# First-group tiles, input order and buffers in a one-core hybrid encoder layer on Trainium2

## The chip, the cores and the metric

The program runs on one core of one Trainium2 chip. The metric is the device time of one execution in microseconds (us), taken as the median of several runs. A core has the engines TensorE (PE, matrix products; PEld is its weight load), VectorE (DVE), ScalarE (ACT), GpSimd (POOL) and SyncE (SP, which here only issues transfers), and 16 DMA engines that serve all queues.

## The reference

One layer for 256 new positions (prompt) and 32 running ones (sample), 288 columns in all, float32, 2048 model channels:

```python
xn   = rmsnorm(x, norm_mix_pre)
proj = xn @ w_in                     # u 1024 | z 2048 | xBC 2560 | dt 32
pool = trailing means of u over windows 2/4/8/16, minus u, @ w_pool per group of 256, * pool_scale
ssd  = Mamba-2 mixer: conv of width 4 and silu on xBC, chunked scan with dt,
       * silu(z), rmsnorm over each of 2 groups of 1024 channels, * ssd_norm
x    = x + rmsnorm(concat[pool, ssd] @ w_out, norm_mix_post)
x    = x + rmsnorm(ConvFFN(rmsnorm(x, norm_ffn_pre)), norm_ffn_post)
```

The outputs are both x and the new histories and states of the pool, the convolutions and the scan.

## The kernel before

**Products.** Activations are kept as 128-channel tiles of 288 columns. Every float32 product is made of three products in a reduced format: weights and activations are each split into a high and a low part, and high x high, high x low and low x high are summed (`mm3`, L162 to L164). ACT makes the high part of the weights (`whi`, L156), DVE the low part (`wlo`, L157), in pieces of 128x1024. `project` (L167) fetches the weights of some output columns (`fetch_w`, L139, on SP), splits them and multiplies; a projection of 256 columns over 16 input tiles is 96 products and four splits on each of ACT and DVE.

**The first group (L217 to L475).** The input isn't there at first, so the kernel starts differently. The 16 input tiles are taken in ten chunks (`CHUNKS`: four of one tile, six of two). For each chunk `first_load` (L238) fetches 800 columns of `w_in` into a slot `raw` (4 slots), with two transfers (L242: B, C and dt; L243: 256 further columns). `prepare` (L363) splits them on ACT (L374, L375) and DVE (L397 for the first four chunks, L388 for the rest), scales and splits the input tile (L372 or L383 on ACT, L390 on DVE), copies it to `xT` (L395) and issues the load of the chunk four further on. For chunks 0 to 3 the input `x0`, `x0s` (512 channels in token order) is turned by PE (`turn_first`, L351, L355, L356); for the others DVE turns it (L378) from `xt`, loaded at L236 and L260. Squares of the input for its norm are taken on ACT with `junk` as their output (L407, L409). The products (L475) go to seven accumulators `first`: 0 and 1 (xs tiles 0 and 1, in the PSUM pool `aux` of three slots), 2 to 5 (B and C) and 6 (dt). `keep_busy` (L337) issues products on a constant tile, whose result is not used: 10 at the start, 5 ahead of the first chunk. Four times parameters are turned by PE through the one `aux` slot left (`columns`, L320) and copied by ACT (L426, L429, L432).

**The rest of the mixer.** `conv_in` (L500) takes a PSUM tile, scaled by the row norm `rstd`, into one of four buffers `ebuf` (L505, L506); `conv_out` (L510) does the convolution and silu on DVE and ACT (L516 to L524). The order in the program is: B, C and xs tiles 0, 1 from the first group; projections xs1 to xs7 (two tiles each), z0 to z7, then u3, u2, u1, u0. Each xs tile goes through `blocks_out` (L195: a DVE transpose into the single buffer `blocks` and four transfers to DRAM) and is read back by `ssd_quad` (L656), which does the scan for four heads at a time. `gate_in` takes z out of PSUM (L771), `gate_mul` (L779) multiplies it in and adds squares to `gsum` on POOL (L762). `rstd_all` sums `gsum` over channels with PE (L740) and makes the group's norm: rg0 for tiles 0 to 7, placed behind z4; rg1 for tiles 8 to 15, placed behind the first u projection.

**The pool mixer.** `pool_in` (L861) takes a u tile into one of four buffers `ubuf` (L864, L865); these are allocated and cleared (L853) after the mixer's buffers are given up. `pool_tile` (L869) makes the window sums and the difference `du`, `pool_group` (L892) multiplies it by `w_pool`. Then the normed xs tiles are split into `mixs` (L124, L125), which take the slots of the 16 `xn` tiles, and `w_out` follows.

**What sets the order.** Each engine works through its instructions in one order. A builder puts them in that order by priority (program order, unless `high_priority` moves them) and by its own simulation of when inputs are ready, so PE instructions of one step can stand inside another's. `pin` keeps an instruction in program order; the whole first group is pinned. In the built program, transfers from SP and ACT share eight completion counters, taken in turn, so an issue waits for the transfer eight before it.

Of the kernel before, what the change touches and what calls it, by code (L numbers as in the profile page):

```python
# [8 lines left out]
F32 = mybir.dt.float32  # L9
F32R = mybir.dt.float32r  # L10
AF = mybir.ActivationFunctionType
ALU = mybir.AluOpType
# [4 lines left out]
P = 128  # L17
# [3 lines left out]
NS = 32  # L21
# [23 lines left out]
CHUNKS = ((0, 1), (1, 1), (2, 1), (3, 1), (4, 2), (6, 2), (8, 2), (10, 2), (12, 2), (14, 2))  # L45
BUSY = 10


@with_exitstack
def body(  # L50
# [57 lines left out]
    def aux(shape, name):  # L108
        return aux_ps.tile(shape, F32, tag="aux", name=name)
# [97 lines left out]
    ones = const.tile([P, P], F32, name="ones")  # L207
    pool.memset(ones, 1.0)
    start = ExitStack()
    xin = start.enter_context(tc.tile_pool(name="xin", bufs=1))  # L210
# [7 lines left out]

    x0 = xin.tile([P, 2, 4 * P], F32, name="x0")
    x0s = xin.tile([NS, 4 * P], F32, name="x0s")  # L220
    xt = xin.tile([P, 9, 3, P], F32, name="xt")
# [16 lines left out]
    def first_load(kb, n):  # L238

        raw = wpool.tile([P, n, NW], F32, tag="raw", name="raw")  # L240
        src = win0[:, kb : kb + n] if kb < 4 else win[:, kb // 4, kb % 4 : kb % 4 + n]
        pin(sp.dma_start(out=raw[:, :, 2 * P :], in_=src[:, :, O_B : O_B + NW - 2 * P]))  # L242
        pin(sp.dma_start(out=raw[:, :, : 2 * P], in_=src[:, :, O_X : O_X + 2 * P]))  # L243
        raws.append(raw)
# [4 lines left out]
    first_input(sp, 0, 0)  # L249
    first_input(act, 1, 0)  # L250
    pin(act.dma_start(out=x0s, in_=x_sample[0, :, 0 : 4 * P]))
    first_load(*CHUNKS[0])
    first_input(sp, 0, 1)
    first_input(sp, 1, 1)
    first_load(*CHUNKS[1])
    first_load(*CHUNKS[2])
# [29 lines left out]
    for i in range(NE):  # L286
# [6 lines left out]
        in_=norm_mix_pre[0, 4 * P :].rearrange("(c p j) -> p c j", p=P, j=4),  # L293
    )
    pb_in = xin.tile([108, P], F32, name="pb_in")
    pool.dma_start(out=pb_in[0:60, :], in_=rows4(state_ssd_conv))
# [37 lines left out]
    def keep_busy(n):  # L334

        for _ in range(n):
            pin(pe.matmul(first[1], busy[:, 0:P], busy, start=True, stop=True))  # L337

    keep_busy(BUSY)
    p_ = aux([P, 4], "pt")  # L340
    pin(pe.transpose(p_, g_in, ident[:4, :4]))
    pin(dve.tensor_copy(g_mix_pre[:, 0:4], p_))
    ssum = xin.tile([P, 12], F32, name="ssum")
    junk = xin.tile([P, 4 * P], F32, name="junk")
    sel4 = xin.tile([P, NS], F32, name="sel4")
# [6 lines left out]
    def turn_first(t):  # L352
        p_ = aux([P, NT], "pt")
        for b in range(2):
            pin(pe.transpose(p_[:, b * P : (b + 1) * P], x0[:, b, t * P : (t + 1) * P], ident))  # L355
        pin(pe.transpose(p_[:, NP_:], x0s[:, t * P : (t + 1) * P], ident[:NS, :NS]))  # L356
        return p_

    def prepare(i, p_=None):
# [6 lines left out]
        tiles = range(kb, kb + n)  # L366
        pieces = (slice(2 * P, NW), slice(0, 2 * P)) if i == 0 else (slice(0, NW),)
        for t in tiles:
# [7 lines left out]
        for t in tiles:  # L376
# [5 lines left out]
            if i:  # L382
                pin(act.activation(  # L383
                    xn[t][:, 0, :], xT[t] if p_ is None else p_, AF.Copy, scale=g_mix_pre[:, t : t + 1]
                ))
        if p_ is None:
            for c in pieces:
                pin(dve.tensor_tensor(lo[:, :, c], raw[:, :, c], hi[:, :, c].bitcast(F32), op=ALU.subtract))  # L388
        for t in tiles:
# [3 lines left out]
            ))  # L393
        if p_ is not None:
            pin(dve.tensor_copy(xT[kb], p_))  # L395
            for c in pieces:
                pin(dve.tensor_tensor(lo[:, :, c], raw[:, :, c], hi[:, :, c].bitcast(F32), op=ALU.subtract))  # L397
        if i + 4 < len(CHUNKS):
# [18 lines left out]
    p_ = turn_first(0)  # L417
    keep_busy(5)
    ahead_w = [prepare(0, p_)]
    for i, (kb, n) in enumerate(CHUNKS):  # L420
# [40 lines left out]
        for q, (r, m, k, x) in enumerate(products):  # L461
            if q == 10 and i < 3:
                ahead_w.append(prepare(i + 1, turn_first(i + 1)))
            if i == 8 and q in (0, 24):
                p_ = aux([P, 3, NF * 2], "ptf")
                for j in range(3):
                    pin(pe.transpose(p_[:, j, :], pf_in[:, q // 8 + j, :], ident[: NF * 2, : NF * 2]))
                pin(act.activation(pf[:, q // 8 : q // 8 + 3, :], p_, AF.Copy))
            if r is None:
                out, c, r = first[6][: 2 * HEADS, :], w[:, k, NW + NB :], 0  # L470
                stop = x == 1
            else:
                out, c = first[m], w[:, k, r * NW + m * P :][:, :P]
                stop = r == 1
            pin(pe.matmul(out, c, xn[kb + k][:, x, :], start=kb + k + r + x == 0, stop=kb + k == KD - 1 and stop))  # L475
# [34 lines left out]
    def conv_out(i, e, out):  # L510
# [13 lines left out]
        dve.scalar_tensor_tensor(out[:, NP_:], th[:, 259:], 1.0, c[:, 259:], op0=ALU.add, op1=ALU.mult)  # L524


    v = mp.tile([HEADS, NT], F32, tag="z", bufs=4, name="v")
# [6 lines left out]

    xs_ps = [first[:2], project(win, [(O_X + 256, 256)], xn, K16, wait=last_split)]
    xT_f = xT_d.rearrange("c p j n -> (c p j) n")
# [274 lines left out]
    for i in range(1, NX // 2):  # L811
        xs_evac(i, xs_ps[i] if i == 1 else project(win, [(O_X + 256 * i, 256)], xn, K16))
        xs_conv(i - 1)
        run_quads(XS_RATE[i])
# [29 lines left out]

    ups = [project(win, [(768, 256)], xn, K16)]
    rg.append(rstd_all(gsum[1], 0.25 / 1024, "rg1"))
    mixer.close()
    outp = ExitStack()
    op_ = outp.enter_context(tc.tile_pool(name="outp", bufs=1))
    ubuf = []  # L850
    for i in range(4):
        e = op_.tile([P, 350], F32, name=f"ubuf{i}")
        pool.memset(e, 0.0)  # L853
        ubuf.append(e)
    uin = {}
    mix = [None] * (NU + NX)
    n_u = [0]
    u_of = {}

    def pool_in(i, p_):  # L860
        u = u_of[i] = ubuf[n_u[0] % 4]  # L861
        n_u[0] += 1
        with tc.high_priority(offset=EVAC):
            dve.tensor_tensor(u[:, 15:271], p_[:, :NP_], rstd[:, :NP_], op=ALU.mult)  # L864
            dve.tensor_tensor(u[:, 286:318], p_[:, NP_:], rstd[:, NP_:], op=ALU.mult)  # L865
        pool.tensor_copy(u[:, 271:286], hist_u[:, :, i])

    def pool_tile(i):
# [185 lines left out]
    x1d = dram.tile([NT, D_MODEL], F32, name="x1d")  # L1054
    outp.close()


# [291 lines left out]
```

## Time and profile before

| what | value |
|---|---|
| median of 3 runs | 1354.79 us (1353.28 to 1355.25) |
| profiled execution | 1361.21 us |
| its span, first to last instruction | 1359.3 us |
| mean granted TensorE clock | 0.997 |
| PE busy in 0 to 66 us | 61.1 us |
| end of the first group's products | 59.4 us |
| DVE busy in 59 to 236 us | 159.7 of 177 us |
| DMA mean rate over the span | 185 GB/s |

Times in the profile count from the first instruction of the profiled execution. A row of the timeline gives start, duration, engine, line, operation, output and inputs, and in brackets how long the engine sat idle before it and what released it. PE's products overlap: the spacing of their starts says how fast PE runs, not their duration. A matmul that is shown with 0.29 us starts 0.131 us after the one before.

### The profile page before, as it was taken

The numbers are of one execution on the slowest core, as the hardware profiler recorded it, in microseconds if no ns is written. First come the engines' busy times: TensorE is split into PE (matmuls) and PEld (weight loads), VectorE is DVE, ScalarE is ACT, GpSimd is POOL, SyncE is SP. The second block draws the span as 40 slices with busy tenths as digits, with TensorE's granted clock in tenths as the row PEclk, the third lists the DMA queues.
The fourth block names the chain that finished last, engine by engine and source line by source line (L and its number), as shares of the span: only waits on it lengthen the run. The fifth ranks groups of instructions, "written<-read, shape, count | busy, mean of one in ns | idle before, by whom it ended". The sixth has DMA issues, their size and how long they took to land.

```text
span 1359.3 us, 25801 instructions
## 1 busy us (share of the span) xinstructions
PE 1342.0 (99%) x10180; PEld 1328.6 (98%) x10180; DVE 889.6 (65%) x1509; ACT 672.6 (49%) x1028; POOL 235.4 (17%) x395
## 2 busy tenths in 40 slices
PE   8999998999999999999999999999999999999997
PEld 7999998999999999999999999999999999999997
DVE  5798889769634469977676653335666666664454
ACT  5755957445544356644544433334444444454443
POOL 3132112111223230211221100000211211101110
PEclk9999999999999999999999999999999999999999
DMA  9878885556755645867555455555455455576763
GB/s 255 259 202 246 267 233 162 170 185 191 222 182 183 191 142 151 250 187 207 160 171 170 150 168 171 164 167 174 157 171 170 158 175 165 159 235 181 196 172 102
DMA packets 302944, 252.13 MB, mean 185 GB/s; under 512 B 74708, under 2 KB 295410, under 8 KB 302822
## 3 DMA queue, kind: packets, MB, share of 16 engines
q1 hardware_dynamic: 300270, 245.63, 59.9%
q0 software_dynamic: 2352, 4.66, 1.2%
q8 instruction: 79, 1.29, 0.4%
q14 instruction: 43, 0.35, 0.1%
q10 hardware_dynamic: 200, 0.20, 0.0%
HBM read 236.13 MB, written 14.31 MB: 184 GB/s over the span
## 4 chain that ended last, share of the span: by engine, by line
PE 91%; DMA 4%; DVE 2%; SPq 1%; issue 1%; ACT 1%; POOL 0%; DVEq 0%; ACTq 0%; POOLq 0%
PE acc L162 29%; PE acc L164 29%; PE acc L163 28%; DMA xs_d<-blocks 2%; DMA raw<-in_w_in 1%; PE acc L475 1%; PE pst L980 1%; SPq L202 1%; PE acc L1255 1%; DVE wlo L157 1%; PE acc_x L475 0%; DMA xt<-in_x_prompt 0%; DMA xk<-xs_d 0%; DVE m L679 0%; PE py L691 0%
## 5 line engine op out<-in xcount | busy, mean ns | idle before, releaser
L157 DVE TENSOR_TENSOR wlo<-raw,whi 128x1024 fp32r<-128x1024 f32 (+1 forms) x402 | 479.8, 1195 | 342.1 <-ACT whi L156 341.0
L156 ACT ACTIVATE whi<-raw 128x1024 fp32r<-128x1024 f32 (+1 forms) x402 | 413.5, 1031 | 481.6 <-PE acc L163 401.6
L162 PE MATMUL acc<-hn,whi 128*128 128x288 f32 x1376 | 404.1, 295 | 0.0
L163 PE MATMUL acc<-hn,whi 128*128 128x288 f32 x1376 | 403.6, 294 | 0.3 <-DVE hn L1039 0.3
L164 PE MATMUL acc<-hn,wlo 128*128 128x288 f32 x1376 | 403.1, 294 | 0.0
L163 PEld LDWEIGHTS acc<-hn,whi 128*128 128x128 f32 x1376 | 259.7, 189 | 0.7 <-DVE hn L1039 0.7
L164 PEld LDWEIGHTS acc<-hn,wlo 128*128 128x128 f32 x1376 | 259.6, 189 | 0.0
L162 PEld LDWEIGHTS acc<-hn,whi 128*128 128x128 f32 x1376 | 257.2, 187 | 0.1
L162 PE MATMUL acc<-fa,whi 128*128 128x288 f32 x682 | 201.9, 296 | 0.0
L163 PE MATMUL acc<-fa,whi 128*128 128x288 f32 x682 | 201.9, 296 | 0.0
L164 PE MATMUL acc<-fa,wlo 128*128 128x288 f32 x682 | 201.5, 295 | 0.0
L164 PE MATMUL acc<-xn,wlo 128*128 128x288 f32 x608 | 179.7, 296 | 1.6 <-DVE wlo L157 1.6
L162 PE MATMUL acc<-xn,whi 128*128 128x288 f32 x608 | 181.1, 298 | 0.2 <-DVE ebuf L506 0.2
L163 PE MATMUL acc<-xn,whi 128*128 128x288 f32 x608 | 180.6, 297 | 0.0
L163 PEld LDWEIGHTS acc<-fa,whi 128*128 128x128 f32 x682 | 128.6, 188 | 0.0
L162 PEld LDWEIGHTS acc<-fa,whi 128*128 128x128 f32 x682 | 128.1, 188 | 0.0
L164 PEld LDWEIGHTS acc<-fa,wlo 128*128 128x128 f32 x682 | 127.9, 188 | 0.0
L164 PEld LDWEIGHTS acc<-xn,wlo 128*128 128x128 f32 x608 | 115.5, 190 | 2.6 <-DVE wlo L157 2.3
L163 PEld LDWEIGHTS acc<-xn,whi 128*128 128x128 f32 x608 | 115.7, 190 | 0.3
L162 PEld LDWEIGHTS acc<-xn,whi 128*128 128x128 f32 x608 | 114.7, 189 | 0.8 <-issue 0.4
L1073 POOL COPY fc_stage<-ebuf 128x4 f32<-128x4 f32 x88 | 27.3, 310 | 496.9 <-DVE ebuf L1072 453.5
L1068 POOL COPY ebuf<-pf 128x2 f32<-128x2 f32 x88 | 72.0, 818 | 129.6 <-DVE fc L1079 58.9
(355 smaller groups left out, 1790.6 us busy)
## 6 DMA issues: line engine op xcount, KB each, us to landing
raw<-in_w_up SPq DMA_DIRECT2D x80, 1024.0 KB, 5.2
raw<-in_w_in SPq DMA_DIRECT2D x76, 512.0 KB, 5.0
raw<-in_w_down SPq DMA_DIRECT2D x32, 1024.0 KB, 5.3
raw<-in_w_out SPq DMA_DIRECT2D x24, 1024.0 KB, 5.5
raw<-in_w_down SPq DMA_DIRECT2D x16, 768.0 KB, 4.8
raw<-in_w_up SPq DMA_DIRECT2D x14, 512.0 KB, 4.4
gb<-g_d SPq DMA_DIRECT2D x8, 832.0 KB, 7.5
raw<-in_w_in SPq DMA_DIRECT2D x6, 544.0 KB, 6.6
```

Source lines behind the costliest of these rows:

```text
L156: act.activation(hi, raw[:, k : k + n, :], AF.Copy)
L157: dve.tensor_tensor(lo, raw[:, k : k + n, :], hi.bitcast(F32), op=ALU.subtract)
L162: then(pe.matmul(out, wh, a[:, 0, :], start=start, stop=False))
L163: then(pe.matmul(out, wh, a[:, 1, :], start=False, stop=False))
L164: then(pe.matmul(out, wl, a[:, 0, :], start=False, stop=stop))
L202: sp.dma_start(out=dv[i], in_=s[32 * i : 32 * (i + 1), :].rearrange("r (j f) -> r j f", f=32))
L475: pin(pe.matmul(out, c, xn[kb + k][:, x, :], start=kb + k + r + x == 0, stop=kb + k == KD - 1 and stop))
L980: ins = pe.matmul(st[:, o, :], x_, btok[:, gi, b, :], start=b != 1, stop=b != 0)
L1068: pool.tensor_copy(e[:, 258:260], pf[:, 4:6, i])
L1073: pool.tensor_copy(fc_stage[:, :, :, i], e[:, 256:324].rearrange("p (s c) -> p s c", c=34)[:, :, 0:2])
L1255: pin(pe.matmul(o, hi, f2[k][:, :, c], start=k == 0, stop=end, skip_group_check=True))
```

## The change

It does these things:

- The 256 further columns that the first group makes are now u tiles 6 and 7 (the pool mixer's last two) and no longer xs tiles 0 and 1. They are taken out of PSUM right behind B and C by `pool_in`, into `ubuf`, which now is allocated and cleared at the start, in a pool of its own that stays open through the mixer. xs0 becomes an ordinary projection; u3 is gone. The pool tiles follow one step earlier: behind u2 come tiles 4, 5 into `ubuf`, then pool tiles 6, 7 and group 3.
- `x0`, `x0s` and `junk` use slots of the weight splits (`hi`, `lo`).
- The second prompt block's first half is issued by SP and not by ACT; both first halves precede all weights, both second halves follow the second chunk's weights.
- `keep_busy`: 11 at the start, 2 behind each of chunk 0's two prompt transposes, 3 behind the turn (18 in all, 15 before). The gains `g_in` are turned into `first[0]` and not into an `aux` slot.
- In `prepare`, chunk 0 is split in three pieces; for chunks 1 to 3 the low weights come ahead of the input's low part and of its copy. The next chunk's turn is asked for behind product 12 of chunk 0 and product 6 of chunks 1 and 2 (before: 10).

```diff
-BUSY = 10
+BUSY = 11
...
+    upool = ExitStack()
+    up_ = upool.enter_context(tc.tile_pool(name="upool", bufs=1))
...
-    x0 = xin.tile([P, 2, 4 * P], F32, name="x0")
-    x0s = xin.tile([NS, 4 * P], F32, name="x0s")
+    x0 = wpool.tile([P, 2, 4 * P], F32, tag="hi", name="x0")
+    x0s = wpool.tile([NS, 4 * P], F32, tag="lo", name="x0s")
...
-        pin(sp.dma_start(out=raw[:, :, : 2 * P], in_=src[:, :, O_X : O_X + 2 * P]))
+        pin(sp.dma_start(out=raw[:, :, : 2 * P], in_=src[:, :, D_POOL - 2 * P : D_POOL]))
...
     first_input(sp, 0, 0)
-    first_input(act, 1, 0)
+    first_input(sp, 1, 0)
     pin(act.dma_start(out=x0s, in_=x_sample[0, :, 0 : 4 * P]))
     first_load(*CHUNKS[0])
+    first_load(*CHUNKS[1])
     first_input(sp, 0, 1)
     first_input(sp, 1, 1)
-    first_load(*CHUNKS[1])
     first_load(*CHUNKS[2])
     first_load(*CHUNKS[3])
...
+    ubuf = []
+    for i in range(4):
+        e = up_.tile([P, 350], F32, name=f"ubuf{i}")
+        pool.memset(e, 0.0)
+        ubuf.append(e)
...
-    p_ = aux([P, 4], "pt")
-    pin(pe.transpose(p_, g_in, ident[:4, :4]))
-    pin(dve.tensor_copy(g_mix_pre[:, 0:4], p_))
+    pin(pe.transpose(first[0][:, 0:4], g_in, ident[:4, :4]))
+    pin(dve.tensor_copy(g_mix_pre[:, 0:4], first[0][:, 0:4]))
...
-    junk = xin.tile([P, 4 * P], F32, name="junk")
+    junk = wpool.tile([P, 4 * P], F32, tag="lo", name="junk")
...
             pin(pe.transpose(p_[:, b * P : (b + 1) * P], x0[:, b, t * P : (t + 1) * P], ident))
+            keep_busy(0 if t else 2)
...
-        pieces = (slice(2 * P, NW), slice(0, 2 * P)) if i == 0 else (slice(0, NW),)
+        pieces = (slice(2 * P, 4 * P), slice(4 * P, NW), slice(0, 2 * P)) if i == 0 else (slice(0, NW),)
...
-        if p_ is None:
+        if i:
             for c in pieces:
                 pin(dve.tensor_tensor(lo[:, :, c], raw[:, :, c], hi[:, :, c].bitcast(F32), op=ALU.subtract))
...
         if p_ is not None:
+            for c in pieces if i == 0 else ():
+                pin(dve.tensor_tensor(lo[:, :, c], raw[:, :, c], hi[:, :, c].bitcast(F32), op=ALU.subtract))
             pin(dve.tensor_copy(xT[kb], p_))
-            for c in pieces:
-                pin(dve.tensor_tensor(lo[:, :, c], raw[:, :, c], hi[:, :, c].bitcast(F32), op=ALU.subtract))
...
-    keep_busy(5)
+    keep_busy(3)
...
-            if q == 10 and i < 3:
+            if i < 3 and q == (6 if i else 12):
                 ahead_w.append(prepare(i + 1, turn_first(i + 1)))
...
+    for i in range(2):
+        pool_in(NU - 2 + i, first[i])
+
-    xs_ps = [first[:2], project(win, [(O_X + 256, 256)], xn, K16, wait=last_split)]
+    xs_ps = [project(win, [(O_X, 256)], xn, K16, wait=last_split)]
...
     for i in range(1, NX // 2):
-        xs_evac(i, xs_ps[i] if i == 1 else project(win, [(O_X + 256 * i, 256)], xn, K16))
+        ps = project(win, [(O_X + 256 * i, 256)], xn, K16)
+        xs_evac(i, ps)
...
-    ups = [project(win, [(768, 256)], xn, K16)]
+    ups = [project(win, [(512, 256)], xn, K16)]
     rg.append(rstd_all(gsum[1], 0.25 / 1024, "rg1"))
...
-    for n, i in enumerate((3, 2, 1, 0)):
+    for n, i in enumerate((2, 1, 0)):
         ps = ups.pop() if n == 0 else project(win, [(256 * i, 256)], xn, K16)
         for j in range(2):
             pool_in(2 * i + j, ps[j])
-        if n:
-            pool_tile(2 * i + 2)
-            pool_tile(2 * i + 3)
-            pool_group(i + 1)
-            for t in range(5 + 3 * n, min(8 + 3 * n, NX)):
-                tc.keep_in_program_order(dve.tensor_tensor(xs[t], xs[t], rg[1], op=ALU.mult))
+        pool_tile(2 * i + 2)
+        pool_tile(2 * i + 3)
+        pool_group(i + 1)
+        for t in range(8 + 3 * n, min(11 + 3 * n, NX)):
+            tc.keep_in_program_order(dve.tensor_tensor(xs[t], xs[t], rg[1], op=ALU.mult))
...
     outp.close()
+    upool.close()
```

`pool_in` itself and the clearing of `ubuf` are only moved up in the program.

More of the change, by code (lines that the diff above doesn't have):

```diff
@@ L524, in conv_out, with pool_in @@
         dve.scalar_tensor_tensor(out[:, NP_:], th[:, 259:], 1.0, c[:, 259:], op0=ALU.add, op1=ALU.mult)
+    n_u = [0]
+    u_of = {}
+    def pool_in(i, p_):
+        u = u_of[i] = ubuf[n_u[0] % 4]
+        n_u[0] += 1
+        with tc.high_priority(offset=EVAC):
+            dve.tensor_tensor(u[:, 15:271], p_[:, :NP_], rstd[:, :NP_], op=ALU.mult)
+            dve.tensor_tensor(u[:, 286:318], p_[:, NP_:], rstd[:, NP_:], op=ALU.mult)
+        pool.tensor_copy(u[:, 271:286], hist_u[:, :, i])
     v = mp.tile([HEADS, NT], F32, tag="z", bufs=4, name="v")
@@ L849, in body @@
     op_ = outp.enter_context(tc.tile_pool(name="outp", bufs=1))
[L850 to L854, printed above, removed]
     uin = {}
     mix = [None] * (NU + NX)
[L857 to L866, printed above, removed]
     def pool_tile(i):
```

## The prediction

> **What bounds the kernel now.** I read the page's busy table first, then the list of waits of TensorE (PE), then its timeline around the longest of them.
>
> ```profile
> span 1359.3 us, 25801 instructions
> ...
> PE 1342.0 (99%) x10180; PEld 1328.6 (98%) x10180; DVE 889.6 (65%) x1509; ACT 672.6 (49%) x1028; POOL 235.4 (17%) x395
> ```
>
> PE is the bound: only 17 us of the span are not busy, and the change leaves every matrix product in place. So it can only give what PE idles, plus what it runs slowly after idling. The waits (total us, times, longest):
>
> ```profile
> PE psum_t L740 <- POOL gsum L762: 3.8, 1, 3.8
> PE acc L475 <- DVE w L397: 1.9, 3, 0.6
> PE acc_x L337 <- DVE busy L213: 1.7, 1, 1.7
> PE acc L164 <- DVE wlo L157: 1.6, 3, 0.8
> PE psum_f L1177 <- ACT fsq L1300: 1.1, 1, 1.1
> ```
>
> The largest is the sum over gate group 0 (rg0). Its timeline (start us, duration):
>
> ```profile
> 233.46 0.29 PE L162 MATMUL acc<-xn,whi 128*128 128x288 f32 x1
> 237.51 1.33 PE L740 MATMUL psum_t<-gsum,ones 128*128 128x288 f32 x2 [3.75 <-POOL gsum L762]
> ...
> 239.12 0.44 PE L162 MATMUL acc<-xn,whi 128*128 128x288 f32 x1
> 239.36 0.44 PE L163 MATMUL acc<-xn,whi 128*128 128x288 f32 x1
> ...
> 242.69 0.29 PE L162 MATMUL acc<-xn,whi 128*128 128x288 f32 x1
> 242.81 0.29 PE L163 MATMUL acc<-xn,whi 128*128 128x288 f32 x1
> ```
>
> Up to 233.46 a product starts every 0.131 us. After the wait it is one per 0.24 us until 242.48, then 0.131 again. From 233.59, when the next was due, to 242.69 are 9.1 us; they hold the sums (0.5 us, by their twin at 292.86) and 17 products (17 x 0.131 = 2.2). **The wait costs 9.1 - 2.7 = 6.4 us**: 3.9 of standing and 2.5 of slow running.
>
> Why is the sum late? Busy time by stretch (length, PE, PEld, DVE, ACT, POOL, granted clock, DMA share, GB/s):
>
> ```profile
> 185.00:210.00 25.00, 23.94 (x195) 22.97 (x194) 22.25 (x41) 12.41 (x28) 2.52 (x4) 1.00 0.82 227
> 210.00:236.00 26.00, 23.19 (x190) 22.23 (x188) 23.36 (x36) 18.61 (x37) 7.73 (x6) 1.00 0.56 164
> ...
> 228.00:241.00 13.00, 8.68 (x50) 7.93 (x49) 12.52 (x15) 7.33 (x12) 5.71 (x4) 0.80 0.41 130
> ...
> 254.00:267.00 13.00, 13.00 (x112) 12.55 (x112) 7.31 (x13) 5.62 (x8) 1.61 (x2) 1.00 0.53 162
> ...
> 306.00:319.00 13.00, 13.00 (x100) 12.98 (x99) 12.05 (x31) 6.97 (x12) 2.30 (x4) 1.00 0.65 205
> ```
>
> From 59 to 236 DVE is busy 159.7 of 177 us (seven such stretches added). It carries a backlog: P(z3) ends near 216 (estimate: P(z4)'s end, below, less 14.7, the spacing of the z projections), but DVE evacuates it at 225.66 and the last addition to gsum ends at 237.46. After 254 the backlog is gone.
>
> **The change, part by part.** I write P(..) for one 256-column projection: 96 products x 0.131 = 12.6 us.
>
> *Order of projections.* Before, the first group makes B, C, dt and xs tiles 0 and 1; then come xs1..xs7, z0..z7, u3..u0. After, the first group makes u tiles 6 and 7 instead, and the order is xs0..xs7, z0..z7, u2..u0. PE's work is equal. Yet z0..z4, and with them the place of rg0, come one projection later: 12.7 us (P(u3) took 280.3 to 293.0). Does DVE's work up to gsum come later too? Hardly. xs tiles 0 and 1 lay finished in PSUM at 59.4, but DVE took them out only at 72.46, since B and C filled the four conv buffers; after the change P(xs0) ends at 72. P(xs2) to P(xs5) were taken out some 3 to 10 us after their end, so DVE may run dry for 3 to 5 us there. Added to DVE are two evacuations of u, 2 x (0.42 + 0.18) = 1.2 us. So gsum is complete near 237.5 + 1.2 + (0 to 4), 239 to 243; by the other way, P(z3) ends near 228.7 and the 11.8 us from its evacuation to gsum (225.66 to 237.46) give 240.5. PE ends P(z4) at 230.7 (22 products ahead of the sums) + 12.7 = 243.4. The sum is ready 0 to 4 us before that: the wait goes, **-6.4 us**. Late next is the wlo wait (1.6 us in all, between 185 and 236, from the same backlog): between 0 and -1.6; I take -0.5, since DVE stays nearly as full.
>
> *The tail.* Behind rg1 there are now two projections (25 us) of cover instead of three for pool tiles, pool groups and mixs splits. DVE was busy 92% from 293 to 345 (48 of 52 us). Without one projection's low parts (4 x 1.22) and two evacuations (1.2) that is 42 us in 39: 3 us too much. The first product on mixs runs at 335.2, its low part was ready at 327.9, so 7 us of slack take it. Cost 0; with the cover gone, up to 12.7 - 7.3 = 5.4 us. The memset of ubuf moves from 293.57 to the start; there P(u2) no longer waits for it, and no PE wait named it: 0.
>
> *The start.* The extra busy products (18 for 15, 0.28 us each = 0.8), filled into the holes at 4.4 to 6.2, should bring the 0.131 us pace, which began at 11.1, forward. The transposes of the next tile are asked for earlier, and low weights precede the input's low part, against the three 0.62 us waits at 13.2, 17.3 and 21.5. From the first product (7.61) to the fifth chunk (24.79) are 17.2 us, holding 80 products (10.5) and three turns (1.4): 5.3 us to win at most. But it isn't the end of this chain:
>
> ```profile
> 31.16 1.54 ACT L374 ACTIVATE w<-raw 128x1600 fp32r<-128x1600 f32 x1 [4.23 <-DMA raw<-in_w_in]
> ...
> 35.41 0.24 ACT L426 ACTIVATE pb<-pt 128x108 f32<-128x108 f32 x1
> ...
> 35.70 0.33 PE L320 MATMUL pt<-ident,pa_in 124*128 124x124 f32 x1
> ```
>
> ACT stood 4.23 us for the seventh chunk's weights, worked through it and three squares without a gap, and freed at 35.65 the one PSUM slot that PE's next transpose needs. PE was there at 35.49. The DMA share is 0.88 to 1.2 from 2 to 38 us: those weights come when the bytes ahead of them are through, and no byte ahead of them is taken away. So whatever PE wins before, it waits out here: 0.2 us to gain, 5.3 if that cover were not there. I take **-0.2**.
>
> *Small pieces, all ahead of 35.7 us.* One input DMA goes from ACT's queue to SP's: the first weights are issued 0.45 us later and land near 6.65, under ACT's xn (to 6.75). The second input halves go behind chunk 1, 2.21 to about 3.6; used at 11.26, 4.3 us after issue would do. A third ACT piece of chunk 0 adds about 0.2 us (a 32-wide one takes 0.22). Four memsets on POOL (1.39) delay the 14 DMAs queued behind them, first used at 29.95. Slots lent to x0, x0s and junk are free by 44.4; the first whi is at 54.2. Together 0.
>
> **Sum**: -6.4 - 0.5 - 0.2 = -7.1 us, against the profiled execution's 1361.2 us (span 1359.3 and 1.9 around it): 1354.1. The median without the profiler is 6.4 us lower, 1354.8. I take the difference over: **1347.7 us**.
>
> **Rivals.** *A, the start counts as well.* If without the profiler those weights land some us earlier, PE is the bound at the start and some 3 of the 5.3 us are kept: 1344.7. For it: PE and ACT meet there within 0.2 us. Against: DMA is full. The row: busy products at 0.28 us from 1.66, a hole at 5.6 to 6.0, full pace at 11.1. The Trainium skill, "TensorE: Matmul & The Clock Gate", Part 1, says that full clock follows about 3.4 us of sustained activity in a free-running window. The trace agrees at both ends: 5 us from the filled stretch at 6.2 to full pace, and slow running after the 3.9 us stand. By the page alone, as an estimate, the pace would come near 6.8 (1.66 and one and a half windows) where it came near 11.3 (6.2 and the same), and half of those 4.5 us, 2.3, would come off the sum.
>
> *B, the rg0 wait travels with z.* It needs P(z3), which also comes 12.7 us later. If DVE runs dry early and its backlog shifts by the whole projection, the wait stays: 1354.8 - 0.2 = 1354.6. For it: the chain through the single blocks buffer takes some 8 us a tile (99.2 to 218.6 for 16). Against: DVE's busy share, above.
>
> *C, slower.* Pool group 3 now follows rg1 in the program with no projection between. Its first product ran 16 us behind rg1's sums (309.0 after 293.0), under P(u2). If PE's order keeps it ahead of P(u1), PE stands those 16 us and runs slowly for 2.5: 1347.7 + 18.5 = 1366; slower from a wait of about 10 us on. Against: at 309.0 those products stand inside the next projection, where their inputs were ready, and rg0's sums 22 products inside P(z5).
>
> **Chances.** Forecast 0.55, A 0.13, B 0.18, C 0.14. Range: 1344.0 to 1356.0; it takes in A, B and the unknown 0 to 1.6 and 0 to 5.4, and leaves out most of C. A measurement of this kernel tells about 0.2% (2.7 us) from no change. Faster by more: 0.68; within: 0.18; slower: 0.14.
>
> **What will show it.** Right: no psum_t L740 among PE's waits, a granted clock of 1.00 where rg0's sums stand, DVE's evacuations at the same times as before while PE is a projection behind, and the pa transpose still near 35.7 behind ACT's pb copy. Wrong: a wait at L740 or at a product on du, mixs or wlo between 290 and 350; the pa transpose well before 35 would be A.

## The result and the profile after

The changed kernel is slower, by less than 2% but clear of the noise: a median of 1366.49 us (1363.12 to 1368.85, 4 runs) against 1354.87 (1353.28 to 1355.25, 4 runs) for the kernel before beside it, a ratio of 1.0086 (95% interval 1.0063 to 1.0109). The profiled execution took 1366.29 us, its span is 1364.6. Run a second time (e9 below) the ratio was 1.0074 (1.0056 to 1.0093). The prediction was 7 us faster; it is 10 to 12 us slower.

The kernel before itself differed from one session to the next (medians of 1354.9, 1359.0, 1357.4, 1357.6 and 1356.5), so below every run is put as a ratio to the kernel before in its own session; 0.0010 of a ratio is 1.36 us. A gain of one run on another is the difference of two such ratios, and both intervals count: taken together (root of the sum of their squares, our estimate) they leave 2 to 3.5 us of doubt in each difference below.

The busy table of the page after, and TensorE's list of waits (total us, times, longest):

```profile
span 1364.6 us, 25783 instructions
...
PE 1340.9 (98%) x10183; PEld 1329.1 (97%) x10183; DVE 892.5 (65%) x1510; ACT 671.7 (49%) x1029; POOL 231.9 (17%) x395
```

```profile
PE acc L162 <- ACT du L120: 6.8, 1, 6.8
PE pt L328 <- ACT pb L434: 3.4, 1, 3.4
PE acc L164 <- DVE wlo L157: 1.9, 1, 1.9
PE acc_x L345 <- DVE busy L215: 1.7, 1, 1.7
PE psum_f L1184 <- ACT fsq L1307: 1.1, 1, 1.1
PE acc L483 <- DVE xn L398: 1.0, 1, 1.0
```

The wait at rg0's sums (3.8 us, the head of the list before) is gone, as forecast. Three others are there: 6.8 us for `du`, 3.4 us for `pb` at the start, and one wait of 1.9 us for `wlo` where there were three of 0.8 at most. The largest, in TensorE's timeline of the kernel after:

```profile
299.82 0.65 PE L762 MATMUL psum_t<-gsum,ones 128*128 128x288 f32 x2
300.30 0.38 PE L863 MATMUL pso<-ident,sc_stage 128*60 128x128 f32 x2
307.51 0.85 PE L162 MATMUL acc<-du,whi 128*128 128x288 f32 x2 [6.83 <-ACT du L120]
308.16 0.44 PE L162 MATMUL acc<-xn,whi 128*128 128x288 f32 x1
308.40 0.44 PE L163 MATMUL acc<-xn,whi 128*128 128x288 f32 x1
```

Two products of pool group 3 stand right behind rg1's sums, ahead of P(u1), whose first two weight pieces of four were split by then (VectorE's low parts at 294.68 and 297.85). Behind the wait a product starts every 0.24 us and not every 0.131. The builder placed the two where `du` isn't ready: its buffers and those of the window sums (`win`) lie in the pool that the program opens behind rg1's sums, and VectorE begins tile 6's window sums at 300.50. Its timeline:

```profile
300.50 0.49 DVE L884 TENSOR_TENSOR win<-ubuf 128x317 f32<-128x317 f32 x1
301.02 1.23 DVE L157 TENSOR_TENSOR wlo<-raw,whi 128x1024 fp32r<-128x1024 f32 x1
302.16 0.49 DVE L884 TENSOR_TENSOR win<-win 128x315 f32<-128x315 f32 x1
302.83 1.95 DVE L769 RECIPROCAL rg<-rg 128x288 f32<-128x288 f32 x1 [0.18 <-ACT rg L768]
...
306.56 0.41 DVE L890 SCALAR_TENSOR_TENSOR dpool<-win,ubuf 128x256 f32<-128x256 f32 x1
```

Where the time went, by milestones of the profiles (start times, us):

| profile | first group ends | rg0's sums | rg1's sums | first `mixs` product | span |
|---|---|---|---|---|---|
| before | 59.39 | 237.51 | 292.86 | 335.19 | 1359.3 |
| after | 60.69 | 244.36 | 299.82 | 339.76 | 1364.6 |

From rg1's sums to the first `mixs` product it now takes 39.9 us with two projections; before it took 42.3 with three, so 42.3 - 12.6 = 29.7 were due. The tail lost 10 us there. From the first group's end to rg1's sums it takes 239.1 with one projection more than before (233.5); 239.1 - 12.6 = 226.5, a gain of 7.0 in these two profiles. The start lost 1.3. Behind the first `mixs` product both take 1024 to 1025 us. The middle stretch differs from one execution to the next, as the next runs show.

### The profile page after: what moved, and what is told of

It reads as the page before. It is cut to its first block, busy times and chain, and to the rows that moved or that the text cites. A ratio compares the mean times of both kernels' runs of the same rounds, so it can differ in the third digit from the quotient of the medians.

```text
span 1364.6 us, 25783 instructions
## 1 busy us (share of the span) xinstructions
PE 1340.9 (98%) x10183; PEld 1329.1 (97%) x10183; DVE 892.5 (65%) x1510; ACT 671.7 (49%) x1029; POOL 231.9 (17%) x395
## 3 DMA queue, kind: packets, MB, share of 16 engines
q1 hardware_dynamic: 300414, 245.76, 59.8%
## 4 chain that ended last, share of the span: by engine, by line
PE 90%; DMA 5%; DVE 2%; SPq 1%; issue 1%; ACT 1%; DVEq 0%; ACTq 0%
PE acc L162 28%; PE acc L164 28%; PE acc L163 28%; DMA xs_d<-blocks 2%; PE acc L483 1%; DMA xk<-xs_d 1%; PE pst L986 1%; DMA raw<-in_w_in 1%; DMA xt<-in_x_prompt 1%; DVE wlo L157 1%; PE acc L1262 1%; SPq L202 0%; PE acc_x L483 0%; DMA xt<-in_x_sample 0%; PE py L713 0%
## 5 line engine op out<-in xcount | busy, mean ns | idle before, releaser
L1086 DVE SCALAR_TENSOR_TENSOR fc<-ebuf,pf,fc 128x290 f32<-128x290 f32 x176 | 90.4, 517 | 3.6 <-ACT fc L1084 1.0
```

The source lines that it names most:

```text
L1086: dve.scalar_tensor_tensor(c, e[:, r_ : r_ + 290], pf[:, r_, i : i + 1], c, op0=ALU.mult, op1=ALU.add)
```

## The experiments

**Which part of the change loses the time.** One session: the kernel before once more; the start alone in the kernel before (input order, `keep_busy`, the order in `prepare`, lent slots); the new order of tiles with the old start (here `x0`, `x0s` and `junk` keep the lent slots for lack of room); the changed kernel with each `pool_group` called one projection later:

```diff
-        pool_group(i + 1)
+        if n:
+            pool_group(i + 2)
...
+    pool_group(1)
     for t in range(NX):
```

> The kernel before, unchanged, profiled once more. Theory: the 3.8 us wait of PE at rg0's sums (L740), with the slow running behind it 6.4 us, was in the one profiled execution (1361.2 us) and is missing in most executions (median 1354.9, 6.4 less): the new profile shows 1353 to 1356 us and no wait, or a wait under 1 us, at L740. Rival: the wait is in every execution and the profiled one was longer for another reason: the wait is there again with 3 to 4 us, and the time is near 1361 in the profile and 1354.9 in the timed runs.

> The kernel before with the change's start alone (input order, busy products, order inside the preparation, slots lent to x0, x0s and junk); xs tiles 0 and 1 stay in the first group, u3 stays last but three. Theory: PE reaches the pa transpose 3.4 us too early, stands behind ACT's pb copy and then runs slowly for some 3 us: the first group ends 1.3 us later than before, 1356.2 us (ratio 1.001). Rival: the start is neutral or a gain, and the whole loss is in the tail: 1351 to 1355.

> The changed kernel with the start of before (input order, 15 busy products, 10 and 5, order inside the preparation); the first group makes u tiles 6 and 7, and x0, x0s and junk keep their lent slots, since they need the room. Theory: 1.3 us less than the changed kernel, 1365.2 us, with the same 6.8 us wait of PE at the first product on du behind rg1's sums, and no wait at rg0's. Rival: start and tail act on each other (DVE later or earlier by the start), the wait at du changes by over 2 us.

> The changed kernel with each pool group called one projection later in the program (group 3 behind P(u1), 2 behind P(u0), 1 behind the last pool tiles), so that P(u1) stands between rg1's sums and the first product on du. Theory: the wait of 6.8 us and the slow running of 2.4 behind it go: 1366.5 - 9.2 = 1357.3 us. Rival: VectorE lacks time in the tail whatever PE's order is; the wait moves to a product on mixs, mixp or wlo, and the time stays above 1363 us.

| run | median us (range, runs) | ratio to before (95%) |
|---|---|---|
| e1, before again | 1358.20 (1354.69 to 1361.31, 12) | 0.9993 (0.9981 to 1.0005) |
| e2, start only | 1357.44 (1352.88 to 1361.30, 12) | 0.9987 (0.9974 to 1.0000) |
| e3, order only | 1366.25 (1364.60 to 1370.43, 6) | 1.0061 (1.0044 to 1.0077) |
| e4, groups late | 1365.87 (1364.48 to 1368.58, 6) | 1.0054 (1.0041 to 1.0068) |

e1: the wait at rg0's sums is there again in the kernel before, so the theory that most executions don't have it fell.

```profile
PE psum_t L740 <- POOL gsum L762: 3.5, 1, 3.5
```

Its stretch from the first group to rg1's sums took 229.9 us, not 233.5: executions of one kernel differ by 3.6 us there, so the gain of 7.0 above is 3.4 by this profile. Put beside the second profile of the changed kernel (e9 below, 243.5 - 12.6 = 230.9) nothing of it is left.

e2 and e3: the loss lies in the order of tiles. The start alone shows no loss (0 to 3.5 us faster by its interval). Over the profiles of this study the first group ends at 57.6 to 61.2 us in the changed order with the new start as it stands (8 profiles, mean 59.5) and at 59.0 to 59.8 with the old start (6, mean 59.3).

e4: the wait for `du` at rg1's sums went, but the time hardly followed: the ratio is below e3's and e9's by 0.0007 and 0.0020, neither clear of the noise. TensorE's waits in e4:

```profile
PE pso L863 <- POOL np_stage L878: 2.7, 1, 2.7
PE acc L164 <- DVE wlo L157: 2.3, 1, 2.3
...
PE acc L163 <- DVE du L121: 1.2, 1, 1.2
```

Everything of the pool mixer now came together ahead of the mixing products; VectorE was busy all of 26 us (busy times per stretch: length, PE, PEld, DVE, ACT, POOL, granted clock, DMA share, GB/s):

```profile
315.00:328.00 13.00, 13.00 (x100) 13.00 (x99) 13.00 (x34) 9.88 (x20) 1.08 (x3) 1.00 0.60 187
328.00:341.00 13.00, 8.32 (x47) 7.44 (x47) 12.99 (x35) 6.24 (x14) 4.54 (x2) 0.74 0.53 170
```

From rg1's sums to the first `mixs` product e4 takes 35.8 us, where 29.7 were due. So putting the products of all three groups later is no cure; the next runs make the work that they wait for earlier.

**Three suspects, one at a time.** Second session: the changed kernel again; ScalarE's copies of `pb`, `pa`, `pc` ahead of `prepare`; the window sums and differences of tiles 6 and 7 during z5 and z6; and, in the kernel before, rg0's sums one projection later.

```diff
 # e5: the three columns(...) blocks come first
+        if i == 5:
+            pb = columns(pb_in, 108, "pb", copies)
...
         if 4 <= i + 1 < len(CHUNKS):
             ahead_w.append(prepare(i + 1))
 # e6: tiles 6, 7 in the conv buffers and in place in ubuf; the split into du stays behind rg1
+        if i in (5, 6):
+            pool_diff(i + 1)
 # e7: kernel before
-        if i == 4:
+        if i == 5:
             rg.append(rstd_all(gsum[0], 0.25 / 1024, "rg0"))
-        if i > 4:
-            for t in range(3 * i - 15, min(8, 3 * i - 12)):
+        if i > 5:
+            for t in range(4 * i - 24, 4 * i - 20):
```

> The changed kernel once more, so that the next three are compared in one session. Both theories: 7 to 12 us above the kernel before, a wait of about 6.8 us of TensorE for du (ACT) behind rg1's sums, a wait of about 3.4 us for pb's copy at pa's transpose near 32 to 35 us, no wait at rg0's sums.

> The changed kernel with ScalarE's copies of pb, pa and pc placed ahead of the next chunk's preparation. Theory (TensorE stands at pa's transpose only because pb's copy stands behind the seventh chunk's high weights in ScalarE's order, and the stand of 3.4 us brings the slow clock): the 3.4 us go or shrink to under 2, the first group ends at 59.5 us or earlier (60.7 in the changed kernel), and the time falls by 1 to 2.5 us against the changed kernel. Rival (the start waits for bytes: the seventh chunk's weights land near 31 us whatever stands ahead of them): the wait moves from the transpose to that chunk's first products, for its weights, the first group ends within 0.4 us of 60.7, and the time stays within 1 us.

> The changed kernel with the windows and differences of pool tiles 6 and 7 worked out during the gates z5 and z6, in the conv buffers and in place in their own buffers; only the split into du is left behind rg1's sums. Takes about 5 us of VectorE out of the tail and leaves du's high part two ScalarE copies behind the opening of the late buffers. Theory (the loss of the change lies in the tail: the du products stand right behind rg1's sums, 6.8 us of wait and some 2.4 us of slow clock after it, and VectorE lacks time behind them): TensorE's wait for du falls to 0.5 to 2 us, no slow clock there, and the time falls by 6 to 9 us against the changed kernel, so that it lies within 3 us of the kernel before. Rival (VectorE's lack of time alone sets the tail; the wait for du is only where it shows): with 5 us of VectorE less the gain is 3 to 5 us, and waits for wlo, du or mixp come up between 310 and 340 us. Second rival (what was moved ahead costs as much there): the gates' stretch gets longer by over 2 us.

> The kernel before with rg0's sums placed one projection later and the eight multiplications by rg0 spread over the last two gates; nothing else is changed. Gives the price of the wait at rg0's sums by itself. Theory (the wait and the slow clock behind it cost what the prediction put down, 6.4 us, of which the profile of the kernel before run again would take 3.5 plus some slow running): no wait at rg0's sums, 4 to 7 us faster than the kernel before. Rival (the wait is slack that the tail gives back: the multiplications by rg0 come later and VectorE is fuller in the last gates, or a part of it is hidden): within 2 us of the kernel before, with new waits for wlo between 260 and 300 us or a later start of the mixing products behind rg1's sums.

| run | median us (range, runs) | ratio to before (95%) |
|---|---|---|
| e9, after again | 1367.73 (1363.47 to 1369.79, 6) | 1.0074 (1.0056 to 1.0093) |
| e5, copies first | 1365.46 (1363.53 to 1365.63, 5) | 1.0060 (1.0043 to 1.0077) |
| e6, sums early | 1364.19 (1360.77 to 1365.73, 5) | 1.0053 (1.0035 to 1.0070) |
| e7, rg0 later (in before) | 1355.04 (1352.01 to 1357.45, 11) | 0.9985 (0.9974 to 0.9996) |

e9 has a wait that the first profile after showed at 1.9 us only. TensorE and VectorE of e9 near 205 us:

```profile
201.34 0.29 PE L163 MATMUL acc<-xn,whi 128*128 128x288 f32 x1
206.43 0.61 PE L164 MATMUL acc<-xn,wlo 128*128 128x288 f32 x1 [4.79 <-DVE wlo L157]
206.83 0.44 PE L162 MATMUL acc<-xn,whi 128*128 128x288 f32 x1
```

```profile
185.11 0.96 DVE L690 TENSOR_TENSOR xw<-xk,tok 128x768 f32<-128x768 f32 x1 [5.66 <-DMA xk<-xs_d]
...
201.61 0.96 DVE L690 TENSOR_TENSOR xw<-xk,tok 128x768 f32<-128x768 f32 x1 [2.62 <-DMA xk<-xs_d]
202.48 1.88 DVE L701 TENSOR_TENSOR m<-m,cbt 128x1664 f32<-128x1664 f32 x1
...
205.16 2.35 DVE L157 TENSOR_TENSOR wlo<-raw,whi 128x1024 fp32r<-128x1024 f32 x2
```

VectorE stands 2.6 us for `xk`, the scan's columns read back from DRAM, with the low weights queued behind it; for the load before, at 185.11, it stood 5.7 us. All six profiles of the changed order up to here (after, e3, e4, e5, e6, e9) have a wait of 1.9 to 4.8 us for `wlo` at this place; those of before, e1 and e2 have none of even 0.9 us.

e5: the wait at the `pa` transpose went, but TensorE stood 2.9 us for `xn` of chunk 4 at 22.5 us instead, and the first group ended at 60.46. Neither side's figures came out whole; the ratio is within the interval of e9. The place where the start stands moves about between executions of identical starts.

e6: the wait for `du` fell from 6.8 to 2.6 us, and the stretch from rg1's sums to the first `mixs` product from 40.0 to 32.9. By the ratios it gained 0.0021 (2.9 us), close to what the first rival gave and not clear of the noise, and its profile has none of that rival's waits between 310 and 340 us. This left the question open; e10 settles it.

e7: with the sums moved, TensorE passes them without a wait, and 2.5 us of wait for `wlo` show at 234.28, where the sums had stood. The gain is 0.0015 (2.0 us, 0.5 to 3.5), not the 6.4 of the prediction: the rival's size, with its wait in another place.

```profile
PE acc L164 <- DVE wlo L157: 2.5, 1, 2.5
```

**The two stands taken away.** Third session. In e10 tiles 6 and 7 are made wholly in z5 and z6, the split into `du` too (two slots of the `b` buffers and one tile in a pool under the mixer's; the late `du` has three buffers, not four). In e11 POOL issues the loads of `xk`. e12 has both; e13 is the kernel before with e7's edit and e11's.

```diff
 # e10, in pool_diff, behind the differences
+        for o, a, m in ((0, 15, 256), (256, 286, 32)):
+            hi, lo = (x[:, o : o + m] for x in uin[i])
+            act.activation(hi, u[:, a : a + m], AF.Copy)
+            dve.tensor_tensor(lo, u[:, a : a + m], hi.bitcast(F32), op=ALU.subtract)
 # e11
-        sp.dma_start(out=xk[:, 0:2, :], in_=xs_d[:NP_, c].rearrange("(b p) c -> p b c", p=P))
-        sp.dma_start(out=xk[:, 2, :], in_=xs_d[TAIL:, c])
+        pool.dma_start(out=xk[:, 0:2, :], in_=xs_d[:NP_, c].rearrange("(b p) c -> p b c", p=P))
+        pool.dma_start(out=xk[:, 2, :], in_=xs_d[TAIL:, c])
```

> The changed kernel with pool tiles 6 and 7 worked out wholly during the gates z5 and z6, the split into du too, in buffers that are open then; one tile of the late du buffers is given up for it. No operation of tiles 6 and 7 is left behind rg1's sums, and group 3's products find their inputs ready. Theory (the tail's loss of 9 us is the stand for du, its slow clock and VectorE's lack of time, all from tiles 6 and 7 being worked out behind rg1's sums): no stand for du at all, the stretch from rg1's sums to the first mixing product falls from 40.0 us to 30 to 32, and the time falls to within 3 us of the kernel before. Rival (a part of VectorE's shortage has nothing to do with these tiles, or the weights of the pool group come late behind rg1's sums): the stretch stays above 33 us, with a wait for wlo or whi behind rg1's sums in place of that for du.

> The changed kernel with the two loads of xk (the token-major columns that each quad reads back) issued by POOL instead of SP. Tests the stand for wlo near 205 us, of 1.9 to 4.8 us in the profiles of the changed order and followed by a slow clock of 0.72: VectorE stands there 2.2 to 2.6 us for xk, whose load is queued on SP right behind two weight loads of 512 KB. Theory (SP's order is the cause): VectorE's waits for xk fall below 1 us, the stand for wlo near 205 us and its slow clock go, and the time falls by 2 to 5 us against the changed kernel. Rival (the load lands late because the DMA engines are full of weights, whichever queue issues it, or VectorE is simply full there): the stand stays above 1.5 us and the time within 1.5 us of the changed kernel.

> Both of the above in one. If the two costs are what they are taken for, their gains add up: 5 to 14 us below the changed kernel, so 0 to 6 us faster than the kernel before. If the stands only move on to the next late thing, the gain is less than that of the better one plus 2 us.

> The kernel before with rg0's sums one projection later (as run already) and xk's loads issued by POOL. With the sums moved, a stand for wlo of 2.5 us with a slow clock of 0.72 showed near 234 us, where the stand for rg0's sums had been. Theory (VectorE is late there in part through its waits for xk): the stand falls below 1 us, the slow clock goes with it, and the kernel is 3 to 6 us faster than the kernel before. Rival (VectorE is full there by its own work, so that some stand near 234 us remains in any case): within 2 us of the kernel with the sums moved alone, that is 1 to 4 us faster than the kernel before.

| run | median us (range, runs) | ratio to before (95%) |
|---|---|---|
| e10, tiles wholly early | 1359.36 (1355.51 to 1361.81, 12) | 1.0012 (1.0000 to 1.0024) |
| e11, `xk` by POOL | 1361.51 (1360.07 to 1364.06, 11) | 1.0031 (1.0020 to 1.0042) |
| e12, both | 1357.24 (1354.68 to 1359.52, 12) | 0.9999 (0.9987 to 1.0010) |
| e13, before, rg0 later, `xk` by POOL | 1352.37 (1351.49 to 1354.24, 8) | 0.9965 (0.9953 to 0.9977) |

e10 settles the tail. Against e9 it gains 1.0074 - 1.0012 = 0.0062, 8.4 us (5 to 11 with both intervals). TensorE behind rg1's sums, and the busy times in 13 us stretches from them (after above, e10 below):

```profile
306.16 0.65 PE L764 MATMUL psum_t<-gsum,ones 128*128 128x288 f32 x2
306.43 0.51 PE L936 MATMUL acc<-du_h,whi 128*128 128x288 f32 x1
306.78 0.30 PE L937 MATMUL acc<-du_l,whi 128*128 128x288 f32 x1
```

```profile
299.82:312.82 13.00, 6.17 (x28) 5.72 (x27) 12.49 (x33) 4.49 (x8) 4.04 (x8) 0.61 0.92 290
312.82:325.82 13.00, 13.00 (x99) 13.00 (x98) 8.79 (x18) 6.17 (x9) 0.69 (x2) 0.99 0.40 115
325.82:338.82 13.00, 13.00 (x100) 13.00 (x99) 13.00 (x31) 11.08 (x23) 0.00 (x0) 1.00 0.72 230
```

```profile
306.16:319.16 13.00, 13.00 (x99) 12.90 (x98) 12.12 (x25) 7.77 (x10) 2.95 (x6) 1.00 1.02 320
319.16:332.16 13.00, 13.00 (x100) 13.00 (x100) 12.83 (x32) 9.07 (x18) 2.56 (x5) 1.00 0.73 226
332.16:345.16 13.00, 13.00 (x101) 12.98 (x100) 13.00 (x27) 8.77 (x18) 3.87 (x5) 1.00 0.48 151
```

With the same products in the same place, but inputs that are ready, TensorE never stops. The stretch to the first `mixs` product is 336.90 - 306.16 = 30.7 us (29.7 were due), against 40.0 in e9. VectorE is at least as full as it was, and that costs nothing: the rival of e4 and first rival of e6, a tail short of VectorE, is not what the changed kernel paid for.

e11 takes the wait near 205 us away. It gains 0.0043 (5.8 us, 3 to 9 with both intervals) against e9. There is no wait for `wlo` left in its list, and VectorE's read of `xk` doesn't stand:

```profile
PE acc L162 <- ACT du L120: 6.8, 1, 6.8
PE acc_x L345 <- DVE busy L215: 1.7, 1, 1.7
PE psum_f L1184 <- ACT fsq L1307: 1.1, 1, 1.1
PE pt L328 <- ACT pb L434: 1.1, 1, 1.1
```

```profile
198.20 0.95 DVE L690 TENSOR_TENSOR xw<-xk,tok 128x768 f32<-128x768 f32 x1
```

But it does not do so by what its theory named, SP's order. A load of `xk` reads two tiles. The second is turned by VectorE (L199) and written by four transfers (L202); the load can't go before they are in DRAM. For the sixth load, VectorE's and SP's rows in e9:

```profile
190.61 0.48 DVE L199 STREAM_TRANSPOSE blocks<-xs 128x288 f32<-128x288 f32 x1 [0.60 <-DMA xs_d<-blocks]
```

```profile
191.12 1.80 SPq L202 DMA_DIRECT2D xs_d<-blocks  x4
193.45 1.22 SPq L139 DMA_DIRECT2D raw<-in_w_in  x2
194.85 0.49 SPq L686 DMA_DIRECT2D xk<-xs_d  x1
```

And in e11 VectorE's, SP's and POOL's:

```profile
184.50 0.47 DVE L199 STREAM_TRANSPOSE blocks<-xs 128x288 f32<-128x288 f32 x1
```

```profile
185.00 2.03 SPq L202 DMA_DIRECT2D xs_d<-blocks  x4
```

```profile
189.71 0.70 POOL L686 DMA_DIRECT2D xk<-xs_d  x1 [5.08 <-DMA xs_d<-blocks]
```

The four writes ahead of the load on SP are those of its own second tile, the twelfth of 16 such groups. What the traces give for this load and the one before (us; a landing that the trace lacks is taken from the read that waited for it; "work" is what VectorE does between turning the second tile and reading the load):

| profile, load | issue behind the last write's landing | issue to landing | instructions and work between | stand at the read |
|---|---|---|---|---|
| before, fifth | 0.1 | 5.1 | 19, 8.9 | 0.8 |
| e9, fifth | 0.6 | 6.9 | 16, 9.8 | 5.7 |
| e11, fifth | 0.5 | 5.1 | 21, 12.2 | 0.2 |
| before, sixth | 0.1 | 4.8 | 17, 9.3 | 0 |
| e9, sixth | 0.7 | 6.7 | 16, 7.7 | 2.6 |
| e11, sixth | 0.9 at most | 7.3 | 22, 12.6 | 0 |

From POOL the load leaves hardly sooner behind its own data than from SP, and it doesn't land sooner as a rule (median 4.6 us from SP in e9, 4.4 from POOL in e11). What differs for both loads is VectorE's order: with the other queue the builder has put at least 31 of VectorE's 1510 instructions in another place, and 2.4 and 4.9 us more of its work now lie ahead of the reads. For the sixth load that is the whole difference; for the fifth, the writes also went out 1.3 us sooner behind the turn and the load landed 1.8 us sooner. No run here changes the queue and keeps VectorE's order, so how the 5.8 us divide is not shown. The Trainium skill, "DMA: Bandwidth & Descriptors", section "Issuing engines are not separate DMA queues", says that issuing from several engines saves only issue time, since all transfers share the same DMA engines. The landing times and the issues above agree.

e12: the two gains don't add up (8.4 + 5.8 = 14.2; against e9 it is 1.0074 - 0.9999 = 0.0075, 10.2 us). TensorE reaches rg0's sums sooner (242.4 us, in e9 246.9) and the wait there is back:

```profile
PE psum_t L764 <- POOL gsum L786: 3.3, 1, 3.3
```

**What rg0's wait is worth.** Last session: e14 is e12 with rg0's sums one projection later; e15 is the kernel before with only `xk` on POOL.

> The changed kernel with tiles 6 and 7 worked out wholly in the gates, xk's loads issued by POOL, and rg0's sums one projection later. Theory (each stand costs what its profile shows, and the 3.3 us at rg0's sums with both other edits are a real cost): no stand over 1 us between 60 and 1340 us, 2 to 5 us faster than the same kernel without the later sums, that is 2 to 6 us faster than the kernel before. Rival (VectorE's work, not the place of the sums, sets how far TensorE gets by 245 us): a stand for wlo comes up in its place, and the time stays within 1.5 us of the kernel before.

> The kernel before with xk's loads issued by POOL, rg0's sums in their place. Theory (the wait at rg0's sums and VectorE's waits for xk are two steps of one chain: the sums wait for the gates' squares, which wait for VectorE, which waits for xk): the wait at rg0's sums falls to 2 us or less, and the kernel is 2 to 4 us faster than the kernel before. Rival (the sums wait for something that xk does not hold up, and TensorE only reaches them earlier): the wait stays at 3 us or more, and the time within 1.5 us of the kernel before.

| run | median us (range, runs) | ratio to before (95%) |
|---|---|---|
| e14, e12 and rg0 later | 1352.88 (1351.12 to 1355.19, 12) | 0.9974 (0.9965 to 0.9983) |
| e15, before with `xk` by POOL | 1353.71 (1352.26 to 1357.70, 12) | 0.9978 (0.9965 to 0.9991) |

In e15 the wait at rg0's sums falls from 3.5 (e1) to 1.9 us without the sums having been moved. The sums wait for the gates' squares and these for VectorE; VectorE's stands for the last two loads of `xk` fall from 2.6 us (before; 2.2 in e1) to 0.2. This edit, too, puts at least 14 of VectorE's instructions in another place, the gates' multiplications among them, so it is likely, but not isolated, that `xk` alone brought the sums forward.

```profile
PE psum_t L740 <- POOL gsum L762: 1.9, 1, 1.9
```

In the kernel before, later sums alone give 2.0 us (e7), `xk` from POOL alone 3.0 (e15), both 4.8 (e13), which are then the whole of it: e13's profile has no stand over 0.9 us between 60 and 1340 us. e14 gains 0.0025 (3.4 us) on e12 and has no such stand either. The two orders of tiles, each rid of its stands, end within 0.0009 of each other, with overlapping intervals, so neither is shown to be the better; e13, the old order, is 0.35% faster than the kernel before (0.23% to 0.47%).

## Why the prediction was wrong

**The tail, put at 0: this step failed**, and by these runs it is the largest part, 8.4 us (e10). The prediction counted VectorE's work (3 us too much, taken by 7 us of slack, 5.4 us at the worst), and nothing speaks against that count: in e10 VectorE is full and nobody waits. What it did not follow through is the order on TensorE. Its rival C had the mechanism (pool group 3's products stay ahead of P(u1)), priced at 16 us plus 2.5 of slow running, and dismissed since the builder puts products where their inputs are ready. It put two of them where the inputs were not. The price was 6.8 us of stand and 2.2 of slow running (20 products at 0.24 us for 0.131, from 308.16 to 312.96). It is not 16 because VectorE begins the window sums 0.7 us behind rg1's sums, where in the kernel before it was 5.0 (297.87), and the first product on `du` runs 7.7 us behind them. "Slower from a wait of about 10 us on" was also too high, because the gain that the wait was to eat was smaller than forecast and the waits for low weights came on top.

**The waits for low weights, put at -0.5: wrong in sign and size.** The edit that removes them is worth 5.8 us in the changed kernel (e11). The prediction took them for a sign of VectorE's backlog of work, which the change leaves nearly as it is. In TensorE's list they go by `wlo`; VectorE's timeline, one step further back, shows an engine that is held by a DMA and not by work: ahead of the read at 185.11 in e9 it is busy 1.46 of 7.10 us.

```profile
178.00:185.10 7.10, 7.10 (x73) 6.64 (x72) 1.46 (x4) 2.19 (x3) 0.90 (x2) 1.00 1.02 312
```

In the changed order the way from the turned tile to the landed load is longer (15.4 us for the fifth load in e9, 10.9 before) with hardly more of VectorE's work in between (9.8 and 8.9). Why it is longer stays open; the DMA engines were full at that time (share 1.02 above).

**rg0's wait, put at -6.4: the wait went, the gain was mis-sized.** Moving the sums alone is worth 2.0 us (e7). The other part of the 6.4 sits in the chain that made the sums late: when TensorE no longer stood at the sums, it stood 2.5 us at `wlo` near the same time. Only both edits together give 4.8 (e13), and that is less than 6.4 as well. The working for the place of the sums was right (rg0's sums at 244.4 without a wait and at a clock of 1.00; forecast 243.4).

**The start, put at -0.2: right in time.** The first group ends where it did (means 59.5 and 59.3), e2 shows no loss, and the time won earlier (chunk 4's first product at 21.2, 24.8 before) is waited out at the `pa` transpose behind ScalarE's copy of `pb`, as the prediction said. That this wait can bring a slow clock of its own was left out (0.72 from 36 to 42 us in the profile after, behind 3.4 us; 1.00 in e9, behind 1.1). Rival A fell.

**The sum.** Tail +8.4, low weights +5.8, rg0 -2 to -4.8 (moved alone, or with `xk` from POOL), start about 0: 9.4 to 12.2, each term with up to 3.5 us of doubt, where 10 to 11.7 were measured. The shift of medians against the profiled execution (6.4 us) played no part. Rival B fell: after the change the sums come without a wait, though the wait came back once the waits ahead of it were taken away (e12).

## What to carry to other kernels

Where a step's own inputs are made only after a buffer opens, look for what the order puts directly behind that opening: a product with late inputs stops an in-order engine, however full of ready work the next step is, and here it was cured by making the inputs earlier (8.4 us), while asking for the products later gave nothing clear of the noise (e4). A wait that names a weight split or a sum is a symptom: go one step back on the releasing engine's own timeline, and expect that taking one wait away shows the next (e7, e12). And an edit that only moves a transfer to another queue can change the order on other engines: before the queue is named as the cause, compare in both traces when the load could go, when it went, when it landed, and how much work lies ahead of its reader.

## What the runs showed of the hardware

The slow running behind a stand comes in pieces. Summed over 6 us windows, (1 - granted clock) x 6 us gives 1.7 us behind the stand of 4.8 us at 206 in e9 (this window alone is below 1.00; the columns are as above):

```profile
200.00:206.00 6.00, 1.64 (x13) 1.40 (x11) 4.39 (x6) 2.07 (x5) 0.22 (x1) 1.00 0.67 191
206.00:212.00 6.00, 5.57 (x30) 5.58 (x31) 6.00 (x11) 2.83 (x3) 0.00 (x0) 0.72 0.72 200
```

Behind the same 6.8 us stand for `du` the sum is 3.4 us in e3 and e11 and 5.1 in after and e9, and 3.4 at rg0's sums before but 1.7 in e1: 1.7, 3.4 or 5.1, that is 3.4 us at half clock, once to three times. A piece that falls into the stand itself costs nothing (of the 5.1 in after, 2.2 fell on products). The Trainium skill, "TensorE: Matmul & The Clock Gate", Part 1, has a clock of one half or full, set by a free-running window of about 3.4 us. The pieces above agree; by that rule one and the same stand costs more or less by where it falls in the window, which no run here shows by itself. Stands of 1.9 to 2.6 us were followed by a slow piece in e15 (1.93), e5 (1.96), e3 (2.00), e4 (2.27) and e7 (2.49), and by none in after (1.92) and e6 (2.59). The same page's Part 1 puts the limit at an idle window of about 3.4 us; by these five rows less is enough. So a stand of 2 us may cost up to 1.7 us more than itself or nothing more; that is part of why executions of one kernel differ by some us.

POOL's copies of 128x30 took 0.25 and 0.27 us in after near 300 us, and 0.62 to 2.64 us in e4 between 315 and 335 us, where VectorE was busy throughout. The 0.62 (at 317.00) is among the latter, so VectorE's busy share alone does not explain the 2.64, and its cause stays open. TensorE's 2.7 us ended with the copy behind it (333.09, 1.90 us).

```profile
330.05 2.64 POOL L878 COPY np_stage<-ubuf 128x30 f32<-128x30 f32 x1 [12.42 <-DVE ubuf L542]
```
